# Low halves of the attention weights taken with a subtraction, and two affine steps moved to ScalarE

## The chip, the cores and the metric

The kernel runs on one core of one Trainium2 chip. Five engines work side by side, each on its own instruction queue: TensorE (PE in the profile, with PEld for the loads of its weights), VectorE (DVE), ScalarE (ACT), GpSimd (POOL) and SyncE (SP, which here only starts DMAs). An engine takes its queue in order: an instruction that waits holds up all behind it. The metric is the device time of one launch in microseconds (us); lower is better.

## The reference

The reference is a two-layer encoder trunk on 1024 tokens of width 1024 in float32. Layer 0 mixes with a convolution branch and a gated branch; layer 1 with differential attention over 8 heads; each layer is followed by a squared-ReLU MLP, and all steps are modulated by a conditioning vector. Cut to what the change touches:

```python
# layer 0, the two branches behind z = h @ w_in
a = conv(a_val * sigmoid(a_gate)) + conv_b            # depthwise, width 31
a = silu(layernorm(a, conv_ln_g, conv_ln_b))          # silu(y) = y * sigmoid(y)
zs = gelu(z_sg); u = zs[..., :512]
v = layernorm(zs[..., 512:], sg_ln_g, sg_ln_b)        # the gate values
sg = u * (einsum('gpq,bnqgc->bnpgc', sg_w, v) + sg_b)
y = concatenate([a, sg]) @ w_out
# layer 1
q, k, v = split(h @ w_qkv, 3)
...
y = o @ attn_w_out
```

## The kernel before

**Matmuls in three passes.** A float32 operand is held as two tiles in a rounded type (`fp32r`): a high half, which is a copy of the value in that type, and a low half, which is what the copy lost. `mm3` (lines 131 to 133) multiplies high by high, high by low and low by high into one PSUM bank. So every weight tile (128 x 1024, 512 KB) has to be brought in and split in two before TensorE can use it.

**Two ways of splitting weights.** In the MLPs, `split` (lines 254 to 256) copies the high half on ScalarE and subtracts it on VectorE. In the other stages `prep` (line 106) does it: SP loads the tile `raw`, ScalarE copies it to `whi` (L112), ScalarE writes minus that copy to `wlo` (L113), and GpSimd starts a DMA that reads the same weights from HBM a second time and adds them onto `wlo` (L114). `Stream` (line 117) calls `prep` some tiles ahead of their use; `raw`, `whi` and `wlo` have three buffers each. `prep` and `Stream` take an argument `eng`, and the attention sets it at some places (`ws.eng = pool`, `wo = Stream(..., eng=pool)`, `wo.eng = None`), but the body of `prep` doesn't read it.

Sixty-one tiles go through `prep`: 4 (`wg`), 8 (`wa`), 8 (`wv`) and 9 (`wo0`) in layer 0, and in the attention 24 of `wqkv` and 8 of `wo1`.

**Layer 0.** TensorE forms the gate and value columns of the convolution branch; L429 and L430 write the padded inputs `ap`. The convolution runs channel group by channel group beside TensorE's next products: VectorE takes 20 taps (L594, L596, added into a PSUM tile `ca`), ScalarE multiplies for the other 11 (L588, L591, two buffers `pr`) and GpSimd adds those up (L592); L597 joins the two sums. In the same time TensorE forms the gate values, ScalarE puts GELU over them (L491, eight tiles `vg` of 128 x 512, tokens on the partitions), and VectorE takes their mean and variance (L493, L494). From the variance, L496 to L503 make the factor `vr`, and **L505** normalises the eight tiles with (value - mean) x factor. TensorE then mixes positions with `sgw` (L523) into PSUM tiles; L526 and L530 on VectorE read those and free their banks. The pool of banks (`mixps`) has six.

Behind that come the statistics over channels (L608 to L615), and for each of eight tiles of the convolution branch: L626 multiplies by the reciprocal deviation, L628 takes the sigmoid of gain x y + bias on ScalarE, **L629** forms gain x y + bias on VectorE, L631 multiplies the two, and `split` makes the operands of the output projection (`project_half`). VectorE adds each projected tile onto the residual (L279). While it does so it also works off products of the conditioning (`mod_unit`, L148), each with a 512 KB DMA ahead of it. L226, L231 and L234 sum the squares for the next norm, and TensorE adds them over the channels (L238).

**Attention.** A generator `qkv(hd)` yields the steps of the projections of one head. The first head's run on their own; those of head hd + 1 are spread over the eight softmaxes of head hd. Three weight tiles a head come from `ws`, one tile ahead. For each block of queries TensorE forms two maps of scores (L957, L958), VectorE adds the bias and takes the row's minimum of the negated scores (L961), ScalarE takes the exponential (L963), VectorE joins both maps (L969 to L972), TensorE transposes the result (L983), ScalarE and VectorE split it (`AT`, L255 and L256), and TensorE multiplies with the values (L994 to L996). `norm` (L1005 to L1013) makes the outputs of a half head, and GpSimd takes the low half of those (`ol`, L256). Beside the last head, `early` already projects four of the eight output tiles, with `wo` on; the other four follow in `project`.

The order in which each engine's instructions stand is worked out when the kernel is built, by a scheduler that simulates the engines' times and goes by the program's order and a few raised priorities.

Of the kernel before, what the change touches and what calls it, by code (L numbers as in the profile page):

```python
# [12 lines left out]
AF = mybir.ActivationFunctionType  # L13
ALU = mybir.AluOpType
# [10 lines left out]
H = 8  # L25
# [15 lines left out]
V_CLG, V_CLB = V_CB + 4, V_CB + 8  # L41
# [6 lines left out]
def trunk(ctx: ExitStack, tc: tile.TileContext, t_in, out):  # L48
    nc = tc.nc
    dve, act, pool, pe, sp = nc.vector, nc.scalar, nc.gpsimd, nc.tensor, nc.sync  # L50

    def f32(ap):
        return ap.bitcast(F32)

    def opened(**kw):
        return tc.tile_pool(reuse_waits="tile", **kw)
# [29 lines left out]
    def load(dst, src):  # L86
        sp.dma_start(out=dst, in_=src)
# [19 lines left out]
    def prep(src, own=None, eng=None):  # L107
        raw = wp.tile([P, D], F32, name="raw", tag="raw", bufs=3)
        load(raw, src)
        hi = (own or wp).tile([P, D], F32R, name="whi", tag="whi", bufs=1 if own else 3)  # L110
        lo = (own or wp).tile([P, D], F32R, name="wlo", tag="wlo", bufs=1 if own else 3)
        act.copy(out=hi, in_=raw)  # L112
        act.activation(out=lo, in_=f32(hi), func=AF.Copy, scale=-1.0)  # L113
        pool.dma_start(out=lo, in_=src, accum_op=ALU.add)  # L114
        return hi, lo

    class Stream:
# [3 lines left out]
        def get(self, i):  # L121
            while self.n < min(len(self.srcs), i + 1 + self.ahead):
                self.got[self.n] = prep(self.srcs[self.n], eng=self.eng)
                self.n += 1
            return self.got[i]
# [9 lines left out]
    def kcol(k):  # L135
        return slice(k * P, (k + 1) * P)
# [36 lines left out]
    def vcol(v):  # L173
        return vec[:, v:v + 1]
# [79 lines left out]
    def split(out_h, out_l, src, lo_eng=None):  # L254
        act.copy(out=out_h, in_=src)  # L255
        (lo_eng or dve).tensor_tensor(out=out_l, in0=src, in1=f32(out_h), op=ALU.subtract)  # L256
# [91 lines left out]
    with opened(name="mix", bufs=1) as mp, ExitStack() as pst:  # L348
# [106 lines left out]
        for j in range(2):  # L455
            dve.tensor_tensor_reduce(out=lv[:, 2 * j, :], in0=lv[:, 2 * j, :], in1=lv[:, 2 * j + 1, :], op0=ALU.mult,
                                     op1=ALU.add, scale=1.0, scalar=0.0, accum_out=ls[:, j:j + 1])
# [18 lines left out]
        vg = []  # L476
        mv = small.tile([P, 8, 2], F32, name="mv", tag="mv", bufs=1)
        vr = small.tile([P, 8], F32, name="vr", tag="vr", bufs=1)
# [20 lines left out]
        vt = small.tile([P, 8], F32, name="vt", tag="vt", bufs=1)  # L499
        dve.tensor_scalar(out=vv, in0=mv[:, :, 1], scalar1=LN_EPS, scalar2=-0.5, op0=ALU.add, op1=ALU.mult)  # L500
        dve.tensor_tensor(out=vt, in0=vr, in1=vr, op=ALU.mult)
        dve.tensor_tensor(out=vt, in0=vt, in1=vv, op=ALU.mult)
        dve.scalar_tensor_tensor(out=vr, in0=vt, scalar=1.5, in1=vr, op0=ALU.add, op1=ALU.mult)  # L503
        for t in range(8):
            dve.tensor_scalar(out=vg[t], in0=vg[t], scalar1=mv[:, t, 0:1], scalar2=vr[:, t:t + 1],  # L505
                              op0=ALU.subtract, op1=ALU.mult)


        ps = bank()
# [1 line left out]
        for g in range(4):  # L511
            dve.scalar_tensor_tensor(out=sgb[:, g, :], in0=ps[:, g * P:(g + 1) * P], scalar=vcol(V_SLB + g),
                                     in1=sgb[:, g, :], op0=ALU.mult, op1=ALU.add)
# [35 lines left out]
        def htile():  # L549
            return (hp.tile([P, C], F32R, name="zh", tag="h", bufs=32),  # L550
                    hp.tile([P, C], F32R, name="zl", tag="h", bufs=32))
# [51 lines left out]
        for c in range(NC):  # L603
            with tc.high_priority(offset=600):
# [5 lines left out]
                for i in range(4):  # L610
                    y = acc[i][:, cs]
# [10 lines left out]
        for c in range(NC):  # L622
            cs = slice(c * C, (c + 1) * C)
            for i in range(4):
                y = acc[i][:, cs]
                dve.tensor_tensor(out=y, in0=y, in1=rs[c], op=ALU.mult)  # L626
                sg = tmp.tile([P, C], F32, name="sg", tag="ht", bufs=3)
                act.activation(out=sg, in_=y, func=AF.Sigmoid, scale=vcol(V_CLG + i), bias=vcol(V_CLB + i))  # L628
                dve.tensor_scalar(out=y, in0=y, scalar1=vcol(V_CLG + i), scalar2=vcol(V_CLB + i),  # L629
                                  op0=ALU.mult, op1=ALU.add)  # L630
                dve.tensor_tensor(out=y, in0=y, in1=sg, op=ALU.mult)  # L631
                z[i][c] = htile()
                split(*z[i][c], y)
# [250 lines left out]
    psum = atps.enter_context(opened(name="atps", bufs=2, space=PSUM))  # L884
    psb.append(psum)
    if True:
        ws = Stream([t_in["wqkv"][m] for hd in range(H) for m in (8 + hd, hd, 16 + hd)], ahead=1)
        SC = -(64 ** -0.5)
        QUOTA = [(2, 3, 0, 0), (2, 2, 2, 1)] * 4
        QUOTA_LAST = [(2, 2, 0, 0), (2, 2, 1, 1)] * 3 + [(0, 2, 0, 0), (0, 4, 0, 0)]  # L890
# [171 lines left out]
        wo = Stream([t_in["wo1"][m] for m in range(KT)], ahead=0, eng=pool)  # L1062
# [54 lines left out]
    with opened(name="wops", bufs=8, space=PSUM) as psum:  # L1117
        psb.append(psum)
        raw = wp.tile([P, 4, P], F32, name="raw", tag="raw", bufs=3)
        for m in range(4):  # L1120
            load(raw[:, m, :], t_in["wo1"][m][:, kcol(KT - 1)])
        w7h = wp.tile([P, 4 * P], F32R, name="whi", tag="whi", bufs=3)
        w7l = wp.tile([P, 4 * P], F32R, name="wlo", tag="wlo", bufs=3)
        split(w7h, w7l, raw.rearrange("p a b -> p (a b)"))
        wo.eng = None
        h = project(wo.get, o, ks8, 2, 3, part=(mid, (w7h, w7l)))
    ast.close()

# [86 lines left out]
```

## Time and profile before

| | |
|---|---|
| time, median of 3 runs | 2307.26 us (2302.62 to 2307.31) |
| the profiled execution's own time | 2306.48 us |
| its span in the profile | 2304.7 us |
| TensorE, VectorE, ScalarE, GpSimd busy | 2194.0, 1817.7, 1233.4, 187.5 us |
| DMA moved | 367.15 MB, of which 31.99 MB on GpSimd's queue |
| layer 0's mixer | 0 to about 345 us |
| first MLP | to about 985 us |
| attention with its projections | to about 1665 us |
| second MLP and output | to the end |

A row of a group of instructions gives line, engine, operation, the tile written and those read, the shapes, how many there were, their busy time in all and the mean in ns of one, and how long the engine sat idle ahead of them and whom it waited for. A row of a timeline gives start and duration in us, and in brackets the idle time ahead. A row of a window gives the stretch, its length, the busy time of PE, PEld, DVE, ACT and POOL with the number of instructions, then the granted TensorE clock (1.00 is full), the busy share of the DMA engines and GB/s.

### The profile page before, as it was taken

To read this page: it belongs to the slowest core of one execution; us is meant where nothing else is said; L and a number is where in the kernel's file an instruction comes from. 1 tells how busy PE (TensorE), PEld (TensorE's weight loads), DVE (VectorE), ACT (ScalarE), POOL (GpSimd) and SP (SyncE) were. 2 spreads that over 40 slices of the span, in tenths; PEclk is the share of its full clock that TensorE was granted. 3 is DMA by queue.
4 is the path that set the end of the run, shared out by engine and by line. 5 is a ranking of instruction groups with operands and counts; after the bars stand their busy time and mean duration, and the time that the engine had idled before them with its cause. 6 is when DMAs were issued, how large, how long until landed. Compare 5 with 4: busy or idle time off the path is not lost.

```text
span 2304.7 us, 27601 instructions
## 1 busy us (share of the span) xinstructions
PE 2194.0 (95%) x10144; PEld 1804.6 (78%) x10144; DVE 1817.7 (79%) x2562; ACT 1233.4 (54%) x1806; POOL 187.5 (8%) x146
## 2 busy tenths in 40 slices
PE   4998989999999999989999999988999999999997
PEld 3776677778888888868888888877778888888886
DVE  7899979995977977978887778874599659578497
ACT  5675536733535435456666666654376354353455
POOL 0485000000000000000000000000000000000002
PEclk9999999999999999999999999999999999999999
DMA  9464674758368275355565644653363561633712
GB/s 350 123 159 101 213 244 148 271 163 304 109 205 288 80 251 198 112 175 84 117 127 106 136 88 90 162 153 88 118 228 112 168 223 47 216 139 111 247 45 73
DMA packets 122646, 367.15 MB, mean 159 GB/s; under 512 B 21552, under 2 KB 24496, under 8 KB 121488
## 3 DMA queue, kind: packets, MB, share of 16 engines
q1 hardware_dynamic: 113728, 333.41, 44.9%
q0 software_dynamic: 8784, 31.99, 7.7%
q8 instruction: 80, 1.31, 0.2%
q14 instruction: 54, 0.44, 0.1%
HBM read 311.77 MB, written 53.58 MB: 159 GB/s over the span
## 4 chain that ended last, share of the span: by engine, by line
PE 74%; DVE 5%; DMA 1%; ACT 1%; issue 1%; DVEq 0%; SPq 0%; ACTq 0%
PE ps L133 21%; PE ps L131 21%; PE ps L132 21%; PE pt L983 2%; PE S L957 2%; PE S L958 2%; PE ps L994 1%; PE ps L995 1%; PE ps L996 1%; DVE b L256 1%; DVE ht L243 1%; DVE wlo L256 1%; DMA w<-sed 1%; PE ps L1007 1%; DMA osp<-oh 0%
## 5 line engine op out<-in xcount | busy, mean ns | idle before, releaser
L132 PE MATMUL ps<-b,whi 128*128 128x512 f32 (+1 forms) x1808 | 699.4, 388 | 4.2 <-DVE b L256 4.1
L131 PE MATMUL ps<-b,whi 128*128 128x512 f32 (+1 forms) x1808 | 691.5, 389 | 6.7 <-ACT b L255 5.4
L133 PE MATMUL ps<-b,wlo 128*128 128x512 f32 (+1 forms) x1808 | 692.6, 388 | 2.2 <-DVE wlo L256 2.2
L255 ACT CAST whi<-raw 128x1024 fp32r<-128x1024 f32 (+1 forms) x225 | 236.5, 1051 | 352.6 <-PE ps L132 320.1
L131 PEld LDWEIGHTS ps<-b,whi 128*128 128x128 f32 x1808 | 340.7, 189 | 78.8 <-ACT b L255 6.2
L132 PEld LDWEIGHTS ps<-b,whi 128*128 128x128 f32 x1808 | 340.2, 188 | 76.8 <-DVE b L256 7.0
L133 PEld LDWEIGHTS ps<-b,wlo 128*128 128x128 f32 x1808 | 339.8, 188 | 72.5 <-DVE wlo L256 3.1
L256 DVE TENSOR_TENSOR wlo<-raw,whi 128x1024 fp32r<-128x1024 f32 (+1 forms) x225 | 274.0, 1218 | 139.1 <-ACT whi L255 137.1
L131 PE MATMUL ps<-hh,whi 128*128 128x512 f32 x576 | 231.0, 404 | 27.3 <-ACT hh L250 15.0
L132 PE MATMUL ps<-hl,whi 128*128 128x512 f32 x576 | 228.5, 398 | 4.9 <-DVE hl L251 4.8
L133 PE MATMUL ps<-hh,wlo 128*128 128x512 f32 x576 | 227.6, 398 | 3.4 <-DMA wlo<-in_wa 3.4
L961 DVE CUSTOM_DVE_ANT_0 L<-S,B 128x1024 f32<-128x1024 f32 x128 | 155.9, 1223 | 46.4 <-PE pt L983 28.9
L744 DVE SCALAR_TENSOR_TENSOR x<-ps,mod,x 128x512 f32<-128x512 f32 x220 | 159.8, 746 | 41.3 <-PE ps L133 40.8
L963 ACT ACTIVATE L<-L,mn 128x1024 f32<-128x1024 f32 x128 | 147.0, 1149 | 81.1 <-DVE mn L961 79.8
L255 ACT CAST b<-f 128x512 fp32r<-128x512 f32 x192 | 118.1, 619 | 76.4 <-PE ps L133 74.7
L131 PEld LDWEIGHTS ps<-hh,whi 128*128 128x128 f32 x576 | 110.5, 192 | 54.5 <-ACT hh L250 17.4
L256 DVE TENSOR_TENSOR b<-f,b 128x512 fp32r<-128x512 f32 x192 | 128.9, 684 | 9.3 <-ACT b L255 9.3
L132 PEld LDWEIGHTS ps<-hl,whi 128*128 128x128 f32 x576 | 110.5, 192 | 31.1 <-DVE hl L251 9.2
L133 PEld LDWEIGHTS ps<-hh,wlo 128*128 128x128 f32 x576 | 110.5, 192 | 28.4 <-DMA wlo<-in_wa 3.9
L148 DVE CUSTOM_DVE_ANT_0 mraw<-mraw,cact 128x1024 f32<-128x1024 f32 x96 | 116.3, 1218 | 10.9 <-DMA mraw<-in_modw 10.9
L733 ACT COPY f<-ps 128x512 f32<-128x512 f32 x96 | 56.2, 589 | 126.1 <-PE ps L133 126.1
L112 ACT CAST whi<-raw 128x1024 fp32r<-128x1024 f32 x61 | 64.0, 1048 | 92.8 <-PE ps L132 78.6
(199 smaller groups left out, 3463.3 us busy)
## 6 DMA issues: line engine op xcount, KB each, us to landing
b<-tspl SPq DMA_DIRECT2D x168, 512.0 KB, 5.2
raw<-in_wm SPq DMA_DIRECT2D x128, 512.0 KB, 4.6
mraw<-in_modw SPq DMA_DIRECT2D x96, 512.0 KB, 4.5
tspl<-b SPq DMA_DIRECT2D x56, 512.0 KB, 5.6
raw<-in_wqkv SPq DMA_DIRECT2D x24, 512.0 KB, 10.2
wlo<-in_wqkv POOLq DMA_DIRECT2D x24, 512.0 KB, 10.2
raw<-in_wo SPq DMA_DIRECT2D x17, 512.0 KB, 4.4
wlo<-in_wo POOLq DMA_DIRECT2D x17, 512.0 KB, 6.9
```

What stands on the lines that cost most here:

```text
L112: act.copy(out=hi, in_=raw)
L131: pe.matmul(ps, wh, ah, start=first, stop=False, skip_group_check=resumed)
L132: pe.matmul(ps, wh, al, start=False, stop=False, skip_group_check=resumed)
L133: newest[0] = pe.matmul(ps, wl, ah, start=False, stop=last, skip_group_check=resumed)
L148: i = dve.tensor_tensor_reduce(out=raw, in0=raw, in1=cact, op0=ALU.mult, op1=ALU.add, scale=1.0, scalar=0.0, accum_out=acc)
L255: act.copy(out=out_h, in_=src)
L256: (lo_eng or dve).tensor_tensor(out=out_l, in0=src, in1=f32(out_h), op=ALU.subtract)
L733: act.copy(out={"X1": c11, "Y1": c22, "X2": c12}[p], in_=ps)
L744: dve.scalar_tensor_tensor(out=x[m][c], in0=ps, scalar=gate(d, m), in1=x[m][c], op0=ALU.mult, op1=ALU.add)
L957: pe.matmul(S[:, sl], self.Q[c][2 * j][:, qs], self.K[j][:, sl], start=True, stop=False)
L961: dve.tensor_tensor_reduce(out=L, in0=S, in1=win, op0=ALU.add, op1=ALU.min, scale=1.0, scalar=3e38, accum_out=mn)
L963: act.activation(out=L, in_=L, func=AF.Exp, bias=mn, scale=-1.0, accum_out=s[:, j:j + 1])
```

## The change

Three edits.

1. `prep` reads `eng`. Where it is set, the low half is `eng`'s subtraction `raw - whi`, and neither ScalarE's negated copy nor the second DMA is issued. It is set to VectorE for `ws` from the start and to GpSimd from the second head on (`ws.eng = pool` stands there already, behind the first head), to GpSimd for the four tiles of `wo` beside the last head, and to VectorE for the four behind them. Layer 0's 29 tiles keep the DMA.
2. The gate values are normalised by ScalarE: VectorE makes the small tile minus mean x factor, and ScalarE forms factor x value + that, for eight tiles.
3. The affine step in front of the swish product (L629) is done by ScalarE.

```diff
@@ prep
         act.copy(out=hi, in_=raw)
-        act.activation(out=lo, in_=f32(hi), func=AF.Copy, scale=-1.0)
-        pool.dma_start(out=lo, in_=src, accum_op=ALU.add)
+        if eng is not None:
+            eng.tensor_tensor(out=lo, in0=raw, in1=f32(hi), op=ALU.subtract)
+        else:
+            act.activation(out=lo, in_=f32(hi), func=AF.Copy, scale=-1.0)
+            pool.dma_start(out=lo, in_=src, accum_op=ALU.add)
         return hi, lo
@@ gate values
         dve.scalar_tensor_tensor(out=vr, in0=vt, scalar=1.5, in1=vr, op0=ALU.add, op1=ALU.mult)
+        dve.scalar_tensor_tensor(out=vt, in0=mv[:, :, 0], scalar=-1.0, in1=vr, op0=ALU.mult, op1=ALU.mult)
         for t in range(8):
-            dve.tensor_scalar(out=vg[t], in0=vg[t], scalar1=mv[:, t, 0:1], scalar2=vr[:, t:t + 1],
-                              op0=ALU.subtract, op1=ALU.mult)
+            act.activation(out=vg[t], in_=vg[t], func=AF.Identity, scale=vr[:, t:t + 1], bias=vt[:, t:t + 1])
@@ swish
-                dve.tensor_scalar(out=y, in0=y, scalar1=vcol(V_CLG + i), scalar2=vcol(V_CLB + i),
-                                  op0=ALU.mult, op1=ALU.add)
+                act.activation(out=y, in_=y, func=AF.Identity, scale=vcol(V_CLG + i), bias=vcol(V_CLB + i))
@@ attention
-        ws = Stream([t_in["wqkv"][m] for hd in range(H) for m in (8 + hd, hd, 16 + hd)], ahead=1)
+        ws = Stream([t_in["wqkv"][m] for hd in range(H) for m in (8 + hd, hd, 16 + hd)], ahead=1, eng=dve)
@@ output projection
-        wo.eng = None
+        wo.eng = dve
```

## The prediction

> **What bounds the kernel now.** I read the page's busy times first, then windows, then the timelines of the places where TensorE waits.
>
> ```profile
> PE 2194.0 (95%) x10144; PEld 1804.6 (78%) x10144; DVE 1817.7 (79%) x2562; ACT 1233.4 (54%) x1806; POOL 187.5 (8%) x146
> ```
>
> That row is the busy times over the span. TensorE is busy 2194.0 of 2304.7 us. The change takes nothing from TensorE, so it can win only what TensorE idles, 110.7 us in all, and the clock that idling costs. The question is which of those gaps the three edits reach.
>
> The largest gap that a moved instruction touches is in layer 0. These are windows of 10 us, then TensorE's, VectorE's, GpSimd's and ScalarE's timelines.
>
> ```profile
> 210.00:220.00 10.00, 7.64 (x59) 7.06 (x57) 9.79 (x10) 2.49 (x3) 0.88 (x1) 1.00 0.60 122
> 220.00:230.00 10.00, 1.16 (x3) 0.97 (x4) 9.79 (x10) 0.00 (x0) 0.00 (x0) 0.56 0.00 0
> 230.00:240.00 10.00, 10.00 (x36) 8.00 (x35) 10.00 (x16) 2.34 (x4) 0.00 (x0) 0.76 0.00 0
> ```
>
> ```profile
> 212.12 5.52 PE L523 MATMUL ps<-sgw,vg 128*128 128x128 f32 x48
> 228.84 0.80 PE L131 MATMUL ps<-hh,whi 128*128 128x512 f32 x1 [11.20 <-DVE tt L526]
> ```
>
> ```profile
> 194.68 0.15 DVE L503 SCALAR_TENSOR_TENSOR vr<-vt,vr 128x8 f32<-128x8 f32 x1
> 194.79 1.29 DVE L596 SCALAR_TENSOR_TENSOR ca<-ap,vec,ca 128x1024 f32<-128x1024 f32 x1
> 195.99 15.04 DVE L505 TENSOR_SCALAR vg<-vg,mv,vr 128x512 f32<-128x512 f32 x8
> 210.96 17.17 DVE L596 SCALAR_TENSOR_TENSOR ca<-ap,vec,ca 128x1024 f32<-128x1024 f32 x13
> 228.04 0.75 DVE L526 SCALAR_TENSOR_TENSOR tt<-ps,vec,sgb 128x512 f32<-128x512 f32 x1
> ```
>
> ```profile
> 195.93 10.19 POOL L592 TENSOR_TENSOR a<-a,pr 128x1024 f32<-128x1024 f32 x4
> 206.67 2.70 POOL L592 TENSOR_TENSOR a<-a,pr 128x1024 f32<-128x1024 f32 x1
> ```
>
> TensorE ends the position products (L523) at 217.64, has filled all six banks, and idles 11.20 us for the first L526 to free one. L526 was late because VectorE's queue held L505 (15.04 us) and thirteen taps (17.17 us) ahead of it. After the gap the clock is low: 0.76 of full over 230 to 240, so 2.4 us of that window are lost, and at about half clock from 228.84 to 230 some 0.6 more.
>
> L505 is slow for a reason that the next rows show: 1948 ns each, where a like form, L629, takes 542.
>
> ```profile
> L505 DVE TENSOR_SCALAR vg<-vg,mv,vr 128x512 f32<-128x512 f32 x8 | 15.0, 1948 | 0.0
> L629 DVE TENSOR_SCALAR a<-a,vec 128x512 f32<-128x512 f32 x8 | 4.3, 542 | 0.1
> L501 DVE TENSOR_TENSOR vt<-vr 128x8 f32<-128x8 f32 x1 | 1.2, 1157 | 1.3 <-ACT vr L497 1.3
> L158 DVE TENSOR_TENSOR mod<-mod,vec 128x1 f32<-128x1 f32 (+1 forms) x26 | 4.0, 155 | 0.0
> ```
>
> While GpSimd adds up its taps, such a VectorE operation ends only with the add; L501 on 8 columns took 1157 ns where L158 takes 155. The taps L596, with one operand in PSUM, ran at their usual length beside the adds.
>
> **The change, part by part.**
>
> *Gate values (edit 2).* It removes 15.04 us from VectorE ahead of the taps. It adds one 128x8 operation like L503, 0.15 us, and on ScalarE eight activations with pointers for both scale and bias. The nearest row is L628, which has both; L250 has one.
>
> ```profile
> L628 ACT ACTIVATE sg<-a,vec 128x512 f32<-128x512 f32 x8 | 6.3, 811 | 1.5 <-DVE a L626 1.4
> L250 ACT ACTIVATE hh<-ht,mod 128x512 fp32r<-128x512 f32 x32 | 22.4, 721 | 23.2 <-DVE ht L243 21.5 <-DVE mod L158 1.7
> ```
>
> So 8 x 0.811 = 6.5 us on ScalarE. Where they can lie:
>
> ```profile
> 198.49 1.15 ACT L591 ACTIVATE pr<-ap,vec 128x1024 f32<-128x1024 f32 x1 [1.19 <-POOL a L592]
> 201.05 1.16 ACT L591 ACTIVATE pr<-ap,vec 128x1024 f32<-128x1024 f32 x1 [1.41 <-POOL a L592]
> 206.88 0.60 ACT L539 ACTIVATE u<-ps 128x512 f32<-128x512 f32 x1 [1.26 <-PE ps L133]
> 212.09 1.04 ACT L112 CAST whi<-raw 128x1024 fp32r<-128x1024 f32 x1 [4.62 <-PE ps L132]
> ```
>
> ScalarE idles 1.19 + 1.41 + 1.26 + 4.62 = 8.5 us between 195 and 212, so 6.5 fit before TensorE asks for the tiles at 212.12. Queued behind them are the multiplications L591: if all eight stand in front, GpSimd's last add moves from 209.37 to at most 215.9, and L597 waits for it; the GELUs L539 free their banks up to 6.5 us later, while TensorE has six.
>
> VectorE then starts the thirteen taps at 196.2 instead of 210.96 and reaches L526 at about 213.4. The first bank has been filled by then (a sixth of 5.52 us past 212.12, 213.0), is free at 214.2, and TensorE wants it at 217.64: the 11.20 us go, and with them the low clock, 3.0 us. **Term: -14.2 us.** Bounds: 0, if something else holds L526, and -14.2.
>
> What is late next? From 228.84 on both TensorE and VectorE move up by nearly the same (14.2 and 14.9 us), so what follows keeps its distances.
>
> *Swish (edit 3).* Eight L629, 4.3 us, leave VectorE; 8 x 0.811 = 6.5 us join ScalarE.
>
> ```profile
> 262.00:333.00 71.00, 70.74 (x307) 57.19 (x305) 59.45 (x98) 31.36 (x39) 4.35 (x5) 1.00 0.86 274
> 333.00:345.00 12.00, 5.32 (x12) 3.57 (x13) 7.93 (x13) 6.90 (x9) 0.86 (x1) 0.72 0.55 173
> 339.69 2.08 PE L238 MATMUL ps<-ss,ones_r 128*128 128x512 f32 x2 [6.95 <-DVE ss L234]
> ```
>
> In that stage TensorE is busy 70.74 of 71 us, so the tiles come in time; ScalarE (31.36 us) has room, and each tile is 0.8 us later than with VectorE. That delay is hidden by TensorE's own work; without that cover it would be 6.5 us. VectorE's L631 now waits for that activation, and the L279 queued behind it, which free TensorE's banks, wait with it. The gap behind it, 6.95 us for the sums of squares at 339.69, has VectorE as its releaser, and VectorE will be up to 0.7 + 4.3 = 5.0 us further ahead. But between 310 and 337 VectorE waits itself for conditioning DMAs and for TensorE, so I count little. **Term: -1 us.** Bounds: -8.7 (the gap and half of the low clock's 12 x 0.28 = 3.4 us, since TensorE idles over half of that window) and +6.5.
>
> *Low halves (edit 1).* 32 of 61 tiles change.
>
> ```profile
> L113 ACT ACTIVATE wlo<-whi 128x1024 fp32r<-128x1024 f32 x61 | 64.2, 1055 | 0.9
> L256 DVE TENSOR_TENSOR wlo<-raw,whi 128x1024 fp32r<-128x1024 f32 (+1 forms) x225 | 274.0, 1218 | 139.1 <-ACT whi L255 137.1
> L592 POOL TENSOR_TENSOR a<-a,pr 128x1024 f32<-128x1024 f32 x40 | 99.3, 2483 | 11.1 <-ACT a L588 4.8 <-ACT pr L591 4.5
> wlo<-in_wqkv POOLq DMA_DIRECT2D x24, 512.0 KB, 10.2
> ```
>
> ScalarE loses 32 x 1.055 = 33.8 us. VectorE gains 8 x 1.218 = 9.7: four tiles of `wqkv` at the entry (three and the one ahead), four of `wo1` at the exit. GpSimd gains 24 x 2.483 = 59.6 and loses 32 issues. 16.8 MB leave the DMA engines. A low half is there about 2.5 us after the high one instead of 1.055 + 10.2 and the issue. `raw` is now held until the subtraction has read it, so SP's next load into that buffer starts up to 2.5 us later, and SP's queue (the copies of Q) stands behind that; with three buffers and one tile ahead I price it at nothing, 24 x 2.5 at worst. GpSimd now waits for the high half, and `ol` and the store of it are queued behind; that store has until the last head.
>
> At the entry:
>
> ```profile
> 988.34 0.50 PE L131 MATMUL ps<-hh,whi 128*128 128x512 f32 x1 [3.00 <-ACT hh L250]
> 986.63 1.04 ACT L113 ACTIVATE wlo<-whi 128x1024 fp32r<-128x1024 f32 x1
> 987.58 1.32 ACT L250 ACTIVATE hh<-ht,mod 128x512 fp32r<-128x512 f32 x2
> ```
>
> L250 stands right behind an L113, so ScalarE gets 1 us earlier; VectorE gets three subtractions, of which one or two fall into the chain of the norm. Bounds -1.0 and +3.7; nearest to one subtraction against one copy: **+0.5 us.**
>
> In the heads:
>
> ```profile
> 1050.00:1500.00 450.00, 448.50 (x2474) 382.38 (x2473) 361.19 (x603) 293.11 (x454) 32.89 (x31) 1.00 0.56 114
> 1159.33 1.05 ACT L112 CAST whi<-raw 128x1024 fp32r<-128x1024 f32 x1 [1.91 <-PE ps L132]
> 1160.42 0.69 DVE L1011 SCALAR_TENSOR_TENSOR v<-ps,w 128x512 f32<-128x512 f32 x1 [1.24 <-PE ps L1007]
> 1165.09 0.15 DVE L972 SCALAR_TENSOR_TENSOR se<-s 128x1 f32<-128x1 f32 x1
> ```
>
> TensorE idles 1.5 us in 450, so there is nothing to win. A GpSimd subtraction behind the cast at 1160.38 would run to 1162.9; from L1011 to L972 VectorE has only operations with an operand in PSUM, like the taps that ran unhindered. **Term: 0**, bounds -1.5 and 24 x 2.483 = +59.6.
>
> The Trainium skill, "SBUF — State Buffer", section "SBUF: two separate sides", speaks against this edit: a VectorE operation with two SBUF inputs and a GpSimd operation that reads SBUF lock each other out for a whole instruction. L505 and L501 agree. By that rule each subtraction that meets L969 to L972 would stop VectorE; it is the third rival below.
>
> At the exit:
>
> ```profile
> 1531.97 0.80 PE L131 MATMUL ps<-th,whi 128*128 128x512 f32 x1 [4.75 <-DMA th<-osp]
> 1616.37 0.79 PE L131 MATMUL ps<-th,whi 128*128 128x512 f32 x1 [6.56 <-DVE v L1011]
> 1600.00:1650.00 50.00, 42.32 (x186) 34.47 (x185) 20.54 (x29) 13.53 (x18) 2.60 (x3) 0.90 0.55 163
> ```
>
> Two gaps, 11.3 us, end on a reload (for the second, the row sums `w` ahead of L1011) while a second copy of a `wo1` tile is under way. At 163 GB/s its 0.52 MB are worth 3.2 us; it shares the engines and is only partly ahead, so I take about a quarter at each gap. **-1.5 us**, bounds -11.3 and +2.5 (GpSimd's `ol` queued behind one subtraction).
>
> **Sum.** -14.2 - 1 + 0.5 + 0 - 1.5 = -16.2 us, from 2306.48 (the profiled execution, of which 1.8 us lie outside its span): 2290.3. The median of the runs shown is 0.8 higher, which makes **2291**.
>
> **Rivals.**
> 1. *The wait moves to ScalarE.* If the scheduler puts the eight activations behind L112 at 212.09, the tiles are ready 6.5 us late for L523, and the short gap brings about 1 us of low clock. For it: ScalarE's queue is full of older work there. Against: 8.5 us of idle time ahead. 2291 + 7.5 = 2298.5. Chance 0.09.
> 2. *The gain is given back at 339.69.* If the conditioning DMAs, not VectorE, set that sum of squares, TensorE waits there for what it has won. For it: VectorE waits for such DMAs just ahead. Against: their buffers are freed by VectorE, which is earlier. About 2306. Chance 0.08.
> 3. *GpSimd's subtractions stop VectorE in the heads* (slower). It takes 16.2 / 24 = 0.68 us of TensorE's time per subtraction to eat the gain; at half a hold, 1.24 us, it costs 29.8: 2321. For it: L505 and L501. Against: today's phase, and GpSimd gives way to a VectorE operation already running. Chance 0.09.
> 4. *The gap at 339.69 closes too*: 2291 - 8.7 + 1 (the term already taken) = 2283.3. Chance 0.12.
> 5. *The edit doesn't do what it says*, because the new order, found by simulation, differs everywhere: contained in the spread of the others.
>
> My forecast, with its neighbours, has 0.62. The range 2281 to 2304 takes in the forecast and rivals 1 and 4. About 0.2% (4.6 us) is what a measurement of this kernel can tell from no change: faster 0.83 (forecast, 1, 4), same 0.08 (rival 2), slower 0.09 (rival 3).
>
> **What the changed profile would show.** L505's line on ScalarE at about 0.81 us; no wait for L526 near 217 and full clock through 240; L526 at about 213. L629's line on ScalarE and the gap at L238 near 325, no longer than 7 us. In the heads, 24 GpSimd subtractions of about 2.5 us and L969 to L972 at their old lengths; longer ones, with new TensorE waits, mean rival 3. GpSimd's queue with about 15 MB. The forecast is wrong if TensorE's busy time changes, or if a gap of over 5 us stands anywhere in 190 to 260.

## The result, and the profile after

The changed kernel takes 2280.87 us (median of 4 runs, 2279.01 to 2283.95) against 2307.28 us before (4 runs, 2302.62 to 2307.42): a ratio of 0.9893, with a 95% interval of 0.9879 to 0.9907. That is 26.4 us faster, where 16 were predicted, and it lies just below the range's lower end of 2281. The profiled execution took 2281.83 us, 24.65 less than that of before. The first row is the page's busy times.

```profile
PE 2193.8 (96%) x10144; PEld 1803.2 (79%) x10144; DVE 1819.4 (80%) x2555; ACT 1214.2 (53%) x1790; POOL 222.3 (10%) x138
```

TensorE's work is the same to 0.2 us; only what it idles and the low clock behind that have shrunk. Where, can be read by lining up the two traces at the n-th matmul. Both have all 10144, and the difference of their start times is TensorE's lead at that place:

| place (n-th matmul, its start before) | lead, us | gained there | predicted |
|---|---|---|---|
| 760, 215.0 us: ahead of the gap of 11.20 us | 0.65 | 0.65 | |
| 800, 235.9 us: behind it | 14.25 | 13.6 | 14.2 |
| 1100, 312.2 us: first statistics done | 7.96 | -6.3 | 0 |
| 3900, 972.0 us: first MLP | 10.65 | 2.7 | 1 |
| 4320, 1078.5 us: entry done | 12.00 | 1.35 | -0.5 |
| 6500, 1475.4 us: end of the heads | 11.77 | -0.2 | 0 |
| 10140, 2293.6 us: end (exit) | 24.94 | 13.2 | 1.5 |

Each trace is one execution. Ahead of the 300th matmul, which no edit reaches, the leads of the runs below differ by up to 4 us, so what counts is the gain from place to place.

So two terms came in as predicted (gate, heads), two were off by 2 us, one gain was partly given back in a place that the prediction had not named, and the exit brought nine times its term.

These are the windows of the changed kernel that answer to the ones shown of before, with the same columns.

```profile
210.00:220.00 10.00, 9.59 (x67) 8.70 (x66) 9.40 (x11) 4.52 (x6) 6.26 (x4) 1.00 0.64 136
220.00:230.00 10.00, 10.00 (x50) 8.29 (x49) 8.34 (x14) 3.35 (x6) 0.00 (x0) 1.00 0.29 75
230.00:240.00 10.00, 4.95 (x16) 2.57 (x15) 6.90 (x12) 4.20 (x7) 0.89 (x1) 0.88 0.90 265
1050.00:1500.00 450.00, 448.50 (x2471) 381.80 (x2470) 365.45 (x602) 276.89 (x437) 66.56 (x31) 1.00 0.43 95
1600.00:1650.00 50.00, 46.55 (x192) 37.16 (x191) 39.35 (x55) 24.05 (x38) 0.00 (x0) 0.94 0.26 103
```

TensorE, 1.16 us busy of 10 in 220 to 230 before, is now busy throughout. In 230 to 240 a new hole stands (4.95 of 10 busy). The heads have the same 448.50 us of 450, with twice the work on GpSimd (32.89 before). TensorE's timeline shows the new hole, a wait for a bank in the output projection (L282 frees it), what is left of the wait for the sums of squares, and the longest wait of the entry:

```profile
238.84 2.07 PE L618 MATMUL ps<-sq,ones_r 128*128 128x512 f32 x2 [5.05 <-ACT sq L617]
313.14 0.79 PE L134 MATMUL ps<-zh,whi 128*128 128x512 f32 x1 [1.70 <-DVE x L282]
329.52 1.13 PE L241 MATMUL ps<-ss,ones_r 128*128 128x512 f32 x2 [0.63 <-DVE ss L237]
979.90 0.80 PE L135 MATMUL ps<-hl,whi 128*128 128x512 f32 x1 [2.66 <-DVE hl L254]
```

**The gate values.** Timelines of VectorE, ScalarE and GpSimd, in this order:

```profile
194.04 0.15 DVE L506 SCALAR_TENSOR_TENSOR vr<-vt,vr 128x8 f32<-128x8 f32 x1
195.35 2.50 DVE L507 SCALAR_TENSOR_TENSOR vt<-mv,vr 128x8 f32<-128x8 f32 x1
215.46 1.23 DVE L600 TENSOR_TENSOR a<-ca,a 128x1024 f32<-128x1024 f32 x1 [0.50 <-POOL a L595]
216.60 1.40 DVE L529 SCALAR_TENSOR_TENSOR tt<-ps,vec,sgb 128x512 f32<-128x512 f32 x2
```

```profile
197.89 5.76 ACT L509 ACTIVATE vg<-vg,vt,vr 128x512 f32<-128x512 f32 x8 [2.76 <-DVE vt L507]
```

```profile
195.29 2.54 POOL L595 TENSOR_TENSOR a<-a,pr 128x1024 f32<-128x1024 f32 x1
```

The eight activations took 5.76 us (6.5 predicted). The one small operation that the edit adds, priced at 0.15 us like its twin L506, took 2.50: it started 0.06 us behind a GpSimd addition and ended with it, at 197.85 against 197.83. ScalarE waited for it, and L529 came at 216.60 and not at 213.4. For the bank that was still in time (TensorE waited 0.41 us).

**The new hole at 233.80.** VectorE's timeline, first of before (L612 is the later L615), then after:

```profile
242.77 1.23 DVE L148 CUSTOM_DVE_ANT_0 mraw<-mraw,cact 128x1024 f32<-128x1024 f32 x1 [1.85 <-DMA mraw<-in_modw]
247.70 2.48 DVE L612 SCALAR_TENSOR_TENSOR a<-ps,a 128x512 f32<-128x512 f32 x4
```

```profile
230.91 1.22 DVE L151 CUSTOM_DVE_ANT_0 mraw<-mraw,cact 128x1024 f32<-128x1024 f32 x1 [2.57 <-DMA mraw<-in_modw]
234.31 1.23 DVE L151 CUSTOM_DVE_ANT_0 mraw<-mraw,cact 128x1024 f32<-128x1024 f32 x1 [1.51 <-DMA mraw<-in_modw]
237.44 2.48 DVE L615 SCALAR_TENSOR_TENSOR a<-ps,a 128x512 f32<-128x512 f32 x4
```

TensorE's squares wait for L615, and L615 stands in VectorE's queue behind four conditioning products (L151), which wait 2.57 and 1.51 us for their loads. Before, four stood there too, with one wait of 1.85 us. SP issues a load when a product has freed its buffer, so the loads moved up with the products: the first product came 12.0 us earlier (225.96 for 237.94), the refill behind it too (227.22 for 239.19). But L615 came only 10.3 us earlier, and TensorE is 14.25 us earlier. Of the 14.9 us that VectorE should have gained, 2.35 went into the small operation, 0.50 into the wait for GpSimd's last add, and 1.6 into the load of the fourth product.

**The exit.** SP's timeline before and then after: the last of a burst of reloads, the store of the outputs `oh` that TensorE needs next, and their reload `th`. (ScalarE had written `oh` by 1515.80 before, 1504.00 after.)

```profile
1519.21 0.41 SPq L87 DMA_DIRECT2D tl<-osp  x1
...
1520.39 0.35 SPq L87 DMA_DIRECT2D osp<-oh  x1
...
1529.18 0.32 SPq L87 DMA_DIRECT2D th<-osp  x1
```

```profile
1502.04 0.38 SPq L87 DMA_DIRECT2D tl<-osp  x1
...
1504.62 0.33 SPq L87 DMA_DIRECT2D osp<-oh  x1
...
1509.39 0.33 SPq L87 DMA_DIRECT2D th<-osp  x1
```

Before, the store went out 4.6 us after its data was there, since SP was still issuing the burst, and the reload followed 8.8 us later. After, it went out at 0.6 us and was followed 4.8 us later. The wait of 4.75 us is gone. The second wait of the exit, 6.56 us behind L1011, is gone too, although VectorE still waits for the row sums `w` (before, then after):

```profile
1615.62 0.69 DVE L1011 SCALAR_TENSOR_TENSOR v<-ps,w 128x512 f32<-128x512 f32 x1 [10.02 <-DMA w<-sed]
```

```profile
1594.63 0.69 DVE L1013 SCALAR_TENSOR_TENSOR v<-ps,w 128x512 f32<-128x512 f32 x1 [6.73 <-DMA w<-sed]
```

TensorE no longer stands behind it. The runs below show why.

### The profile page after: what moved, and what is told of

The parts are those of the page before. It is cut to its first block, busy times and chain, and to the rows that moved or that the text cites. A ratio compares the mean times of both kernels' runs of the same rounds, so it can differ in the third digit from the quotient of the medians.

```text
span 2279.8 us, 27567 instructions
## 1 busy us (share of the span) xinstructions
PE 2193.8 (96%) x10144; PEld 1803.2 (79%) x10144; DVE 1819.4 (80%) x2555; ACT 1214.2 (53%) x1790; POOL 222.3 (10%) x138
## 5 line engine op out<-in xcount | busy, mean ns | idle before, releaser
L114 POOL TENSOR_TENSOR wlo<-raw,whi 128x1024 fp32r<-128x1024 f32 x24 | 64.3, 2680 | 1058.0 <-PE S L960 684.6
L259 DVE TENSOR_TENSOR b<-f,b 128x512 fp32r<-128x512 f32 x192 | 129.7, 690 | 10.3 <-ACT b L258 10.3
L151 DVE CUSTOM_DVE_ANT_0 mraw<-mraw,cact 128x1024 f32<-128x1024 f32 x96 | 116.6, 1222 | 12.6 <-DMA mraw<-in_modw 12.6
```

The lines of the kernel that those rows point to most:

```text
L114: eng.tensor_tensor(out=lo, in0=raw, in1=f32(hi), op=ALU.subtract)
L151: i = dve.tensor_tensor_reduce(out=raw, in0=raw, in1=cact, op0=ALU.mult, op1=ALU.add, scale=1.0, scalar=0.0, accum_out=acc)
```

## The experiments

Each time stands beside runs of the kernel before on the same chip; a ratio is to those, with its 95% interval.

### One edit at a time

`e1_gate` is before with edit 2 alone, `e2_swish` with edit 3 alone, `e3_low` with edit 1 alone.

> The kernel before with the gate values on ScalarE alone (edit 2). Theory: the eight VectorE operations stood ahead of L526, and their 15 us are worth 11.2 us of TensorE's idle time and 3 us of low clock at 218 us, of which some 6 are given back near 234, where TensorE waits for the squares behind VectorE's conditioning products. So TensorE is 14 us ahead at 222 us, 8 ahead at 245, and the whole is 8 to 11 us faster (2296 to 2299). Rival: the give-back belongs to the swish edit or to the other order of the whole change; then this kernel keeps 14 us (2293). Second rival: nothing is kept, because the next norm waits for the conditioning DMAs; then 2305.

> The kernel before with the affine step of the swish on ScalarE alone (edit 3). Theory: TensorE is busy for 70.7 of 71 us while these eight stand, so they are worth at most 1 us: 2306 to 2308. Rival: they are what closes the 6.95 us gap at the sums of squares (340 us), by taking 4.3 us from VectorE; then 2299 to 2302, with that gap under 3 us.

> The kernel before with the low halves by subtraction in the attention alone (edit 1). Theory: the gain of the whole change behind the heads is this edit's: 13 us at the exit (the gaps of 4.75 and 6.56 us and their low clock) and 1 at the entry, so 2290 to 2294, layer 0 as before. Rival: the exit's gaps closed because the work arrives in another order after the earlier stages moved; then this kernel is within 4 us of before.

| | time, us | ratio | less, us |
|---|---|---|---|
| gate values | 2290.28 (5 runs) | 0.9932 (0.9911 to 0.9954) | 15.7 |
| swish | 2297.57 (10 runs) | 0.9964 (0.9953 to 0.9974) | 8.4 |
| low halves | 2297.38 (10 runs) | 0.9958 (0.9946 to 0.9971) | 8.6 |
| all three | 2280.87 (4 runs) | 0.9893 (0.9879 to 0.9907) | 26.4 |

None of the three times lies in a range that was expected of it: the gate values brought more, the swish more than even its rival, the low halves less. The parts add up to 32.7 us, 6.3 more than the whole, so some waits are counted twice. Leads by place, worked out as above: the low halves are 2.1 us behind at the end of the heads, 1.8 of it already at the 300th matmul, and gain 11.0 at the exit, so the exit is theirs. The swish gains 5.3 us where the sums of squares are (1100th to 1200th matmul; TensorE's wait there is gone) and 3.4 at the entry, where it moved nothing. With the gate values alone 4.93 us of that wait for the sums of squares are left. Each of the three runs closes a wait of 2.25 us for the scores at the entry (1027.51 before). Gate and swish have no work there, and no run shows why it goes. Neither of these two takes away the first wait of the exit, but both take away the second, which they don't touch either, and in both a third one comes up in its place. In the gate run's timeline of TensorE:

```profile
1523.71 0.80 PE L131 MATMUL ps<-th,whi 128*128 128x512 f32 x1 [5.31 <-DMA th<-osp]
```

```profile
1629.19 0.79 PE L133 MATMUL ps<-th,wlo 128*128 128x512 f32 x1 [4.75 <-DMA wlo<-in_wo]
```

The last row is the wait for a low half that is still being fetched the second time: the thing that edit 1 removes.

### Low halves of the eight wo1 tiles alone

The changed kernel's edit 1, without edits 2 and 3, and with the `wqkv` tiles back on the DMA:

```diff
-        ws = Stream([t_in["wqkv"][m] for hd in range(H) for m in (8 + hd, hd, 16 + hd)], ahead=1, eng=dve)
+        ws = Stream([t_in["wqkv"][m] for hd in range(H) for m in (8 + hd, hd, 16 + hd)], ahead=1)
...
-        ws.eng = pool
```

> The kernel before with subtraction for the eight tiles of wo1 alone; the 24 of wqkv keep the negated copy and the second DMA. Theory: the second reads of wo1 (4.2 MB) stand in front of the small transfers of the exit (store and reload of the head's output, row sums), so the eight tiles alone bring 12 to 15 us: 2292 to 2295, both gaps at the exit under 1 us. Rival: it is the scheduler's order or ScalarE's time in the heads, to which wqkv's tiles belong; then 0 to 3 us and both gaps stay.

2301.85 us (10 runs), ratio 0.9984 (0.997 to 0.9998): 4.2 us less, where 12 to 15 were expected. The first wait of the exit goes with these eight tiles; the second stays, on the same releaser:

```profile
1606.42 0.79 PE L134 MATMUL ps<-th,whi 128*128 128x512 f32 x1 [4.53 <-DVE v L1014]
```

So the transfers of the `wqkv` tiles have no part in the first wait, and removing transfers doesn't by itself remove the second.

### What the second wait of the exit is

The traces keep which engine's signal an instruction waits for. Before, the first product of the exit (L131, right behind the last L1007 in TensorE's queue) waits for VectorE; that is the row with 6.56 us for L1011. In the gate run's timeline the same product follows at once:

```profile
1599.69 1.12 PE L1007 MATMUL ps<-sq,ones_r 128*128 128x512 f32 x2 [1.12 <-ACT sq L1005]
1600.25 0.80 PE L131 MATMUL ps<-th,whi 128*128 128x512 f32 x1
```

The order is the same, and the wait is not. The pool of the exit takes over the attention's banks, and its first tile may or may not fall on the bank that L1011 has still to read. The wait for VectorE is there before, in the run on eight tiles and in the run `e8_null` below, and those three show the gap; it is missing in the gate, swish and low-half runs and in the changed kernel, and those four don't. To try the bank alone:

```diff
     with opened(name="wops", bufs=8, space=PSUM) as psum:
         psb.append(psum)
+        dve.memset(bank()[:, 0:1], 0.0)
```

> The kernel before, with one column of the first PSUM bank of the exit written by VectorE, so that the first product of the exit falls on the next bank. Nothing else is moved. In the program of before this product (L131 behind the last L1007) waits for VectorE; in those of the three runs in which the 6.56 us wait went, and of the changed kernel, it has no wait for VectorE, and here neither. If that bank is the cause, the 6.56 us wait behind L1011 goes with its low clock, and the time is 2296 to 2300; if, as in the gate and the swish run, a wait of nearly 5 us for the second copy of a wo1 tile takes its place, 2301 to 2304. Rival, that the bank is of no account: the wait stays, 2305 to 2309.

2304.45 us (10 runs), ratio 0.9984 (0.9972 to 0.9995). The wait behind L1011 went: TensorE is 8.85 us further ahead at the 7200th matmul than at the 7100th. A hundred matmuls on, 8.0 of it are lost, on the low half of a `wo1` tile:

```profile
1640.82 0.79 PE L133 MATMUL ps<-th,wlo 128*128 128x512 f32 x1 [5.09 <-DMA wlo<-in_wo]
```

So two causes stand one behind the other. Taking the transfers away and leaving the bank keeps 4.53 us; moving the bank and leaving the transfers keeps 5.09 us; only edit 1 whole, which happens to do both, gets the 11.0 us.

### A new order without moved work

```diff
+        dve.scalar_tensor_tensor(out=vt, in0=mv[:, :, 0], scalar=-1.0, in1=vr, op0=ALU.mult, op1=ALU.mult)
         for t in range(8):
             dve.tensor_scalar(out=vg[t], in0=vg[t], scalar1=mv[:, t, 0:1], scalar2=vr[:, t:t + 1],
                               op0=ALU.subtract, op1=ALU.mult)
```

> The kernel before, with only the one 128x8 operation of the gate part added on VectorE (0.15 us, its result read by nobody). No work is moved. If the new order that any small edit brings is worth time by itself, the waits of 2.25 us at the entry (K) and 6.56 us at the exit (L1011), which went in both the gate and the swish run, go here too, and the time is 2298 to 2303. Rival, that the order is of no account: 2305 to 2309, both waits in place.

2306.21 us (10 runs), ratio 1.0002 (0.9992 to 1.0011): no difference, and both waits in place. The order isn't worth time by being new. It is worth time where it moves a tile to another bank, as above.

### Is the first wait of the exit the traffic?

The changed kernel, with GpSimd also issuing the old transfer of every `wo1` tile, into a spare tile that nothing reads:

```diff
             eng.tensor_tensor(out=lo, in0=raw, in1=f32(hi), op=ALU.subtract)
+            if dead is not None:
+                for n in range(NC):
+                    pool.dma_start(out=dead, in_=src[:, n * C:(n + 1) * C], accum_op=ALU.add)
```

> The changed kernel, with the eight wo1 tiles still subtracted, but GpSimd also issues the old accumulating transfer of each such tile (two halves of 256 KB) into a spare tile that nothing reads. If the reload of the last head's values waits at the exit because these transfers share the DMA engines, the wait for th<-osp (4.75 us before, gone after) comes back at 3 to 6 us, the store osp<-oh takes 7 us or more again, and the time is 2285 to 2290. Rival, that it was the low half coming late or another order of the queues: no such wait, stores at 3 to 4 us, 2279 to 2283.

2304.18 us (10 runs), ratio 0.9988 (0.9979 to 0.9998): 23 us more than without, far beyond what was expected of either theory. The run answers another question than the one it was made for. TensorE waited 16.85 us for `th<-osp` at 1541.92; GpSimd's timeline shows what held it:

```profile
1544.35 0.87 POOL L117 DMA_DIRECT2D dead<-in_wo  x1 [3.58 <-DMA dead<-in_wo]
1548.87 0.86 POOL L117 DMA_DIRECT2D dead<-in_wo  x1 [3.65 <-DMA dead<-in_wo]
1553.06 0.86 POOL L117 DMA_DIRECT2D dead<-in_wo  x1 [3.32 <-DMA dead<-in_wo]
1553.62 1.59 POOL L263 TENSOR_TENSOR ol<-osb,oh 128x512 fp32r<-128x512 f32 x1
```

All transfers write the same tile, so each issue waits for the one before to land, and the subtraction of `ol` is queued behind them. With two spare tiles in turn:

> As the run before it with the dead transfers, but they alternate between two spare tiles, so that no issue on GpSimd has to wait for the landing of the one just before (there GpSimd stood 3 to 7 us at each issue, with the subtraction of ol queued behind, and the wait for th<-osp grew to 16.85 us). If the traffic itself delays the reload at the exit, a wait of 3 to 6 us for th<-osp is left, osp<-oh takes 7 us or more, and the time is 2285 to 2290. Rival, that only GpSimd's queue counts: no wait for th<-osp over 1.5 us, 2279 to 2284.

2290.35 us (4 runs), ratio 0.9927 (0.9904 to 0.995), 9.5 more than the changed kernel. A wait of 4.83 us for `th<-osp` is back, at 1548.10, but again GpSimd's queue made it. `oh` was stored at 1542.18, and SP's queue (first row: the store of `ol`) waited for GpSimd, whose `ol` ran only at 1547.62, behind issues that waited for a landing:

```profile
1549.24 0.32 SPq L87 DMA_DIRECT2D osp<-ol  x1
1549.65 0.38 SPq L87 DMA_DIRECT2D th<-osp  x1
```

That is the second such reload. At the first, the one that was late before, the reload followed its store after 6.1 us (1506.44 to 1512.52; 4.8 in the changed kernel, 8.8 before), and TensorE waited 0.27 us. But this doesn't settle the traffic. TensorE came late to that reload itself: it had waited 3.26 us up to 1509.00 for `vT`, which shares its buffers with `osb`, so that ScalarE could write it only when `ol` had been taken (1508.33), again behind an issue that waited. Of the 9.5 us some 5.7 were lost in that stretch (6500th to 6800th matmul). And 6.1 us is no sign of traffic: in the run of the low halves alone, which has no second copies at all in the attention, the same reload followed its store after 6.2 us (1518.27 to 1524.48), in the run on eight tiles after 5.05. In the five kernels that keep the second copies of `wo1` (before, gate, swish, `e8_null`, `e11_bank`) it took 8.4 to 8.9 us.

### Does GpSimd have room in the heads?

```diff
-            eng.tensor_tensor(out=lo, in0=raw, in1=f32(hi), op=ALU.subtract)
+            for _ in range(2 if eng is pool else 1):
+                eng.tensor_tensor(out=lo, in0=raw, in1=f32(hi), op=ALU.subtract)
```

> The changed kernel with each of GpSimd's 24 subtractions done twice, 24 x 2.68 = 64 us more on GpSimd in the heads. If the heads have slack for them (two of VectorE's long operations there read PSUM, and GpSimd is busy a tenth of the time), the time stays within 2279 to 2284. By the third rival of the prediction (each subtraction stops VectorE on the path) at a quarter of a hold, 0.62 us for each, it is 2281 + 15 = 2296, and TensorE gets waits of over 1 us between 1050 and 1500.

2301.58 us (10 runs), ratio 0.9986 (0.9977 to 0.9995): 20.7 us more than the changed kernel. The third rival was right about the mechanism. TensorE's lead on the changed kernel goes from 3.8 us at the 4320th matmul to 19.3 us of delay at the 6800th: 23.1 us for the 20 added subtractions that lie between, 1.2 us each. First the window of the heads (TensorE 448.50 before), then one of the two groups of VectorE that grew (L215 in the changed kernel, 693 ns in its heads; the other is `osb`, L1015 there, from 752 to 1772 ns), then one of its operations and GpSimd beside it:

```profile
1050.00:1500.00 450.00, 434.12 (x2361) 366.47 (x2360) 374.45 (x572) 262.74 (x415) 108.37 (x48) 0.99 0.37 87
```

```profile
L216 DVE TENSOR_TENSOR ln<-r 128x512 f32<-128x512 f32 x13 | 24.8, 1908 | 0.4
```

```profile
1078.94 2.00 DVE L216 TENSOR_TENSOR ln<-r 128x512 f32<-128x512 f32 x1
```

```profile
1075.50 4.89 POOL L115 TENSOR_TENSOR wlo<-raw,whi 128x1024 fp32r<-128x1024 f32 x2 [29.48 <-ACT whi L112]
```

GpSimd's second subtraction ends at 1080.39; L216, 0.69 us long on its own, starts 1.45 us ahead of that and ends 0.55 us behind it.

### The hole at 233.80

The eight products behind the gate columns, ordered behind the first half's sums of squares (`lasts[0]`, the last L618 of that half):

```diff
-        queue_mod(0, [16])
+        queue_mod(0, [16], lasts[0])
```

> The changed kernel, with the eight conditioning products for the gate columns (L151, about 10 us of VectorE with their waits for DMA) ordered behind the sums of squares of the first half. If the new wait at 233.80 (5.05 us, and some 3 us of low clock) comes from VectorE standing in these products ahead of L615, it shrinks below 2 us, TensorE is 5 to 8 us further ahead at 250, and the time is 2274 to 2278. Rival, that the next thing is late instead: the updates of x (L282) wait for the gate columns, TensorE runs out of banks near 260 to 275, and the time is 2280 to 2288.

2289.07 us (4 runs), ratio 0.9926 (0.9911 to 0.9941): slower than the changed kernel by 8. Both theories held, one after the other. The hole went and TensorE was 7.6 us ahead at the 920th matmul, so the products were its cause; then it had no bank, because the updates of `x` need all eight columns:

```profile
276.90 0.79 PE L134 MATMUL ps<-zh,whi 128*128 128x512 f32 x1 [14.14 <-DVE x L282]
```

Finishing the columns in pairs lets the first updates go after two products:

```diff
-        queue_mod(0, [16], lasts[0])
+        for n in range(16, 24):
+            background.append(lambda n=n: mod_unit(0, n, lasts[0]))
+            if n % 2:
+                background.append(lambda n=n: mod_fin(0, n - 1, n + 1))
```

> The changed kernel with the eight conditioning products behind the first half's sums of squares, as in the run before it (whose wait at 233.80 went, 7 us ahead at 241, and which lost it and 9 us more at 262.76, where TensorE waited 14.14 us for a bank), but with the gate columns finished in four pairs, so that the first updates of x need two products and not eight. If the wait at 262.76 came from the updates standing behind the last product, no wait over 3 us stands between 225 and 290, TensorE is 5 to 8 us ahead of the changed kernel at 300, and the time is 2274 to 2278. Rival, that the lead is lost at the sums of squares behind it (311 to 355): 2279 to 2283.

2279.95 us (4 runs), ratio 0.9882 (0.9862 to 0.9902), not to be told from the changed kernel: the rival held. No wait over 1.5 us between 225 and 290 is left, TensorE is 11.0 us ahead of the changed kernel at 306 us, and loses 10.6 of it here:

```profile
326.73 2.08 PE L241 MATMUL ps<-ss,ones_r 128*128 128x512 f32 x2 [8.81 <-DVE ss L237]
```

VectorE stood at a product again in between:

```profile
306.73 1.23 DVE L151 CUSTOM_DVE_ANT_0 mraw<-mraw,cact 128x1024 f32<-128x1024 f32 x1 [4.63 <-DMA mraw<-in_modw]
```

So the products' place alone doesn't decide it. What is left to try is their supply, 24 loads of 512 KB through two buffers. The convolution has left two tiles free by then:

```diff
+        def spare(n):
+            return mp.tile([P, D], F32, name="mraw", tag="cv", bufs=6) if n % 2 else None
...
-            background.append(lambda n=n: mod_unit(0, n, lasts[0]))
+            background.append(lambda n=n: mod_unit(0, n, lasts[0], spare(n)))
...
-        queue_mod(1, [8, 0], conv_end)
+        for n0 in (8, 0):
+            for n in range(n0, n0 + 8):
+                background.append(lambda n=n: mod_unit(1, n, conv_end, spare(n)))
+            background.append(lambda n0=n0: mod_fin(1, n0, n0 + 8))
```

> The run with the products behind the sums of squares and the columns in pairs (7 to 11 us ahead of the changed kernel between 240 and 307 us, all of it lost in a wait of 8.81 us for the layer's last sums of squares at 317.91), with one more thing: every second conditioning product of the first layer loads into one of the two tiles that the convolution has left free, so that up to four loads are under way and not two. If VectorE lost the lead by standing in its queue for these loads (4.63 us at 302), the wait at 317.91 shrinks below 3 us, TensorE keeps 5 us or more at 400, and the time is 2268 to 2275. Rival, that the loads share the DMA engines with the first MLP weights and the reload of x, so that more of them at once are each later: the wait stays at 6 us or more, 2278 to 2283.

**2270.31 us** (5 runs, 2267.84 to 2270.83), ratio 0.9836 (0.9823 to 0.985): faster than both kernels. The wait at 317.91 is gone and TensorE keeps 11.85 us in the first MLP over the changed kernel. These are the products between 220 and 345 us in the changed kernel (with what VectorE waited for ahead of them) and here:

```profile
L151 DVE CUSTOM_DVE_ANT_0 mraw<-mraw,cact x24: 1211/1220/1227, 226.0 to 325.6; 128x1024 f32<-128x1024 f32 x24
...
  DMA mraw<-in_modw: 11.3, 7
```

```profile
L151 DVE CUSTOM_DVE_ANT_0 mraw<-mraw,cact x24: 1204/1212/1220, 241.6 to 300.4; 128x1024 f32<-128x1024 f32 x24
```

The last product starts 25 us earlier, although the first starts 16 us later, and VectorE has no wait for a load left there. With the place as in the run before, it was the supply.

## Why the prediction came out low

**Gate values, -14.2: right.** 13.6 us, by the mechanism given (L505 leaves VectorE's queue, the taps move up, the bank comes free). Inside it one price was wrong, 2.50 us for 0.15. At the bank the cover took it up (L529 was 3.2 us later than predicted and TensorE waited 0.41 us), further on it was missing. The prediction had quoted the row that showed this (L501, 1157 ns on 8 columns) and then priced the new operation by L503.

**"What follows keeps its distances": wrong.** The reason given was that TensorE and VectorE move up together. They didn't move up by the same: at L615 VectorE was 10.3 us ahead and TensorE 14.25, for the three reasons given above, and with the low clock (0.88 over 230 to 240) 6.3 us were given back. A gap of over 5 us between 190 and 260 was one of the forecast's own signs of being wrong, and this one has 5.05. The second rival named waits for these loads, but 100 us further on and for the whole gain. That VectorE's standing in the products made the hole is shown by the run that moved them.

**Swish, -1: too small.** The wait for the sums of squares shrank from 6.95 to 0.63 us, as the fourth rival had it, and the edit alone closes it and brings 5.3 us there. A wait of 1.70 us for a bank ahead of it is new. In the changed kernel 2.7 us of layer 0 remain behind the give-back.

**Entry, +0.5: wrong sign, 1.35 us gained.** The sum was not what its words say: one subtraction against one copy is 1.218 - 1.055 = 0.16 us, not 0.5. The subtractions do cost: in the run of the low halves alone TensorE's other waits of the entry (those over 0.5 us from 970 to 1060) grew from 6.3 to 9.4 us. What the term left out is the wait of 2.25 us for the scores, which went, as it does with the gate or the swish edit alone; so the low halves alone came out 0.2 us behind. The sign turned by that wait, for no reason that the prediction gave.

**Heads, 0: right, and by less than it looked.** The prediction argued from today's phase, and it is the phase that holds. Where a subtraction meets one of VectorE's long operations with two SBUF operands, it is GpSimd that waits:

```profile
1088.10 1.28 DVE L973 SCALAR_TENSOR_TENSOR L<-L,rs 128x1024 f32<-128x1024 f32 x1
```

```profile
1088.40 3.26 POOL L114 TENSOR_TENSOR wlo<-raw,whi 128x1024 fp32r<-128x1024 f32 x1 [6.64 <-ACT whi L112]
```

VectorE was first by 0.3 us, kept its 1.28 us, and GpSimd took 3.26 us where it takes 2.41 beside operations that read PSUM. In the doubled run, where GpSimd was first, VectorE paid, and the price of 1.2 us each is near the half hold of 1.24 us that the third rival put down. The Trainium skill, "SBUF — State Buffer", section "SBUF: two separate sides", says that of the two whichever starts first keeps the shared port for its whole instruction; the rows agree in both directions (3.26 and 2.00 us). The prediction counted L505 to the operations with two SBUF inputs; it reads one tile and two columns, and was held all the same (1948 ns for 542). One of VectorE's operations did not keep its old length: the one of 128x1 that writes `se` took up to 0.79 us beside GpSimd's `ol`, for 0.15, and TensorE didn't wait for it.

**Exit, -1.5: the step that failed.** It measured 13.2 us, beyond even its bound of 11.3. The term took a quarter of the bandwidth's worth of one second copy at each gap. Three things were wrong with that. The first wait came through a chain on SP: a store that stood 4.6 us behind a burst of reloads and was then followed by its reload only after 8.8. The second was no matter of transfers to begin with, but of the bank on which a new pool's first tile falls. And the bound left out the low clock behind both gaps, which the swish's bound had counted: the lead grew by 7.3 us at the first gap (4.75 us of waiting, then a clock of 0.83 from 1532 to 1542) and by 8.8 at the second (6.56, then 0.76 from 1616 to 1626); the start of the second MLP then took 3.0 back.

What stays open is how the first wait divides. The run on eight tiles shows that it goes with the `wo1` tiles; whether by the transfers, by ScalarE's saved copies or by the order of SP's queue around the burst, no run moved alone. Nor was it tried which of the edits' changes of order shifts the bank.

## What to carry to other kernels

A gain on one engine lasts only to the next thing that didn't move by as much: before counting it through, work out by how much each engine moves, look for work in the same queue that waits for loads, and how many buffers supply those. A wait for a bank at the start of a new pool can be an accident of allocation; read in the trace what the instruction waits for, and ask what stands right behind the wait before pricing it. Work put on GpSimd beside VectorE costs by phase, not by length: 24 subtractions were free, and 20 more in the same stretch cost 1.2 us each.

## What the hardware showed

- An operation of VectorE on 128x8 values with two SBUF operands took 2.50 us beside a GpSimd addition and its twin 0.15 us without: here the hold lasted to the end of the addition, however small the operation. In the run with two spare tiles one of 128x1 took 4.34 us (from 1504.01): it began during a DMA issue of GpSimd and ended with the second of the two GpSimd subtractions behind that.
- GpSimd's subtraction of 128x1024 takes 2.40 us alone, 3.26 to 3.37 where VectorE is in first; VectorE does the same in 1.22.
- Eight activations of 128x512 with pointers for scale and bias take 5.76 us back to back, 0.72 each, against the group's mean of 0.80, since their records overlap.
- In the run with one spare tile, where each issue of a DMA on GpSimd has to wait until its target has been written, GpSimd stood 2 to 7 us at most of them, with the subtraction queued behind.
